# A hybrid decoder layer: constant matmuls ahead of the first product, and another order at its end

## The chip, the core and the metric

The kernel runs on one core of a Trainium2 chip. Its time is device time in microseconds (us) of one execution; the time before is the median of three executions, 1987.16 us (1986.9 to 1989.67). The profile is of one more execution, which took 1982.96 us.

The engines are named as in the profile. PE does matmuls, and PEld loads their stationary operand. DVE works elementwise with up to two tensor operands, ACT elementwise with one operand and a function, POOL here makes a sum over partitions. SP only issues transfers (SPq in the timeline).

## The reference, cut to what matters

```
mod = (silu(c) @ w_ada + b_ada).reshape(B, 6, D)
sh1, sc1, gt1, sh2, sc2, gt2 = mod
h    = rmsnorm(x, g_norm_mix) * (1.0 + sc1) + sh1
proj = h @ w_in
q, k, v, xr, xg = split(proj)          # 1024 columns each
...                                    # attention of q, k, v; recurrence of xr, gated by xg
x = x + gt1 * (mixed @ w_out)
x = x + gt2 * (square(relu(h2 @ w_mlp_in)) @ w_mlp_out)
return rmsnorm(x, g_norm_final)
```

x has 512 tokens of 2048 features, w_in is 2048 x 5120. Only the first two products of w_in are of interest here: the one that makes xr (the first product) and the one that makes the first two heads of q and k and the first four of v (the second).

## The kernel before

Features lie on the 128 partitions and tokens on the free axis, so the 2048 features are 16 **blocks** (k from 0 to 15). Every f32 operand is split into a high half, rounded to the type the matmul takes, and a low half, the difference; ACT makes the high half and DVE the low half. A product of two split operands takes three matmuls: weight high by x high (line L259), weight high by x low (L262), weight low by x high (L263), in the helper `mm3`. A block of a product is 8 outputs of 3 matmuls of 128x512, which is 24, and each output has one of the eight PSUM banks.

**The first product** (the loop over k behind `banks = ...`) multiplies w_in's columns for xr by x times g(1 + sc1), without the norm's factor for each token: that factor (r1) and the shift are put in later, in `conv`. In block k the program names the work for block k+1:

- `weights1(k + 1)`: two transfers of 256 KB on SP (L236), two copies on ACT (L244) and two subtractions on DVE (L122). The transfers are pinned, and the rest has an urgency of up to 150.
- `load_x`: a block of x of 256 KB (L372), its square on ACT (L361) and the running sum `acc` on DVE (L362). In the kernel before it runs two blocks ahead up to k = 4, and three from there.
- `prep1(k + 1)`: a row of sc1, which is a product of a row of w_ada with silu(c) and its sum, done on DVE in two halves of 1024 columns (L211) and put together in L220; then the scale (L380), the high half of x on ACT (L382) and the low half on DVE (L383). The row products load the next rows, 512 KB a half, on SP (L199, pinned).
- at k = 12 the norm starts: POOL sums `acc` over the partitions (L336). At k = 14 ACT and DVE make r1 of it (L345 to L354). Both are marked with an urgency of 250.

**The second product** takes h itself, with norm and shift. `prep2(k)` makes its operand: a row of sh1 (L211, L220), scale and norm on DVE (L389), high half on ACT (L391), low half on DVE (L392). `prep2(0)` and `prep2(1)` are named in block 15 of the first product, and each further one two blocks ahead. Its weights come by `weights` without a pin. Its banks are those of the first product, which ACT empties first (L443).

What sets the order on each engine: the framework walks the whole program in its own estimate of time, and gives an engine the ready instruction that stands earliest in the program. `high_priority(offset=n)` moves an instruction n places forward in that rank, and `later(ins)` pins it behind the instruction that the program names before it on the same engine. Engines work in the order that this makes, also when on the chip the next one is not ready and a later one is. So an instruction on ACT that waits for a transfer holds up all that stands behind it.

At the very start two matmuls with one row of the operand spread c over the partitions (L176), and ACT takes silu of it (L177).

Of the kernel before, what the change touches and what calls it, by code (L numbers as in the profile page):

```python
# [12 lines left out]
AF = mybir.ActivationFunctionType  # L13
ALU = mybir.AluOpType
PSUM = bass.MemoryType.PSUM

P = 128
S = 512
D = 2048
NK = D // P  # L20
HEADS = 8
AW = 1024
# [19 lines left out]
URGENT = 150  # L42
EVAC = 88
PAD, SHIFT = 8, 16

# [17 lines left out]
def hybrid_layer_kernel(  # L65
# [32 lines left out]
    def T(tag, dt=F32, cols=None):  # L98
        return new(next(split_tag) if tag == "w4" else tag, dt, cols)
# [6 lines left out]
    def bank(tag):  # L106
        count[0] += 1
        return pp.tile([P, S], F32, tag=tag, name=f"ps_{tag}_{count[0]}", bufs=PBUFS[tag])

    def const(cols, name, dt=F32):  # L110
        return sp.tile([P, cols], dt, tag=name, name=name)

    act = nc.scalar.activation
    stt = nc.vector.scalar_tensor_tensor
    tt = nc.vector.tensor_tensor
    mm = nc.tensor.matmul

    def f32(ap):
        return ap.bitcast(F32)

    def low(out, full, high):
        tt(out=out, in0=full, in1=f32(high), op=ALU.subtract)  # L122

    def split(full, tag):
        h = T(tag, F32R)
        act(h, full, AF.Copy)
        lo = T(tag, F32R)
        low(lo, full, h)
        return h, lo
# [3 lines left out]
    ones, ntri, nones_r = const(P, "ones"), const(P, "ntri", F32R), const(P, "nones_r", F32R)  # L133
# [14 lines left out]
    def col(base, j):  # L148
        return vec[:, base + j : base + j + 1]
# [15 lines left out]
    nc.vector.memset(ones, 1.0)  # L165
    nc.vector.memset(eps, EPS)


    crow = T("tt")
    nc.sync.dma_start(crow[0:1, :1024], c[:, 1024:])  # L170
# [2 lines left out]
    for i in range(2):  # L173
        v = slice(i * S, (i + 1) * S)
        ps = bank("mm")
        mm(ps, ones[0:1, :], crow[0:1, v], start=True, stop=True)  # L176
        act(cb[1][:, v], ps, AF.Silu)  # L177

    def later(ins):
        return tc.keep_in_program_order(ins)  # L180


    def mod(m, j):
        return mods[:, m * NK + j : m * NK + j + 1]
# [42 lines left out]
    tags2 = [MID]  # L227


    def weights(src, tag=None, urgent=URGENT, pin=False):  # L230

        n = src.shape[-1] if len(src.shape) == 2 else src.shape[1] * src.shape[2]
        with tc.high_priority(offset=urgent):
            r = T("wr" if tag not in ("w3", "w4", "ts") else "raw")
            dst = r[:, :n] if len(src.shape) == 2 else r[:, :n].rearrange("p (a b) -> p a b", b=src.shape[2])
            dma = nc.sync.dma_start(dst, src)  # L236
            if pin:
                later(dma)
            if tag in ("w4", "ts"):
                both = T(tag, F32R)  # L240
                h, lo = both[:, :S], both[:, S : 2 * S]
            else:
                h, lo = T(tag or "wh", F32R), T(tag or "wl", F32R)
            act(h[:, :n], r[:, :n], AF.Copy)  # L244
            low(lo[:, :n], r[:, :n], h[:, :n])
        return h, lo

    class Half:
# [9 lines left out]
    def mm3(out, wh, wl, ah, al, start, stop, pin=False, **kw):  # L258
        first = mm(out, wh, ah, start=start, stop=False, **kw)  # L259
        if pin:  # L260
            later(first)
        mm(out, wh, al, start=False, stop=False, **kw)  # L262
        mm(out, wl, ah, start=False, stop=stop, **kw)  # L263

    def blk(o):
        return slice(o * P, (o + 1) * P)


    class Lane:
# [8 lines left out]
        def next(self):  # L278
            if not self.queue:
                return False  # L280
            try:
                self.wait += next(self.queue[0]) or 0.0
            except StopIteration:
                self.queue.pop(0)
            return True
# [47 lines left out]
    def rnorm_steps(accs, n, ptag, tok=slice(0, S), r=None):  # L333
        m = T("n")[:, tok]
        if ptag is None:
            nc.gpsimd.partition_all_reduce(m, accs[0][:, tok], channels=P, reduce_op=bass_isa.ReduceOp.add)  # L336
            ps = m
        else:
            ps = (bank(ptag) if accs else ptag)[:, tok]
            for i, acc in enumerate(accs or []):  # L340
                mm(ps, ones, acc[:, tok], start=i == 0, stop=i == len(accs) - 1)
        yield
        r_ = T("n") if r is None else r
        r = r_[:, tok]
        ins = act(r, ps, AF.Ln, bias=eps[:, 0:1], scale=1.0 / n)  # L345
        if ptag is None:
            later(ins)
        ins = nc.vector.tensor_scalar(out=m, in0=ps, scalar1=1.0 / n, scalar2=EPS, op0=ALU.mult, op1=ALU.add)
        if ptag is None:
            later(ins)  # L350
        act(r, r, AF.Exp, scale=-0.5)
        tt(out=m, in0=m, in1=r, op=ALU.mult)
        stt(out=m, in0=m, scalar=-0.5, in1=r, op0=ALU.mult, op1=ALU.mult)
        stt(out=r, in0=m, scalar=1.5, in1=r, op0=ALU.add, op1=ALU.mult)  # L354
        yield r_
# [11 lines left out]
    xs, xhl, hT = {}, {}, {}  # L367

    def load_x(k):
        xs[k] = T("a")  # L370
        with tc.high_priority(offset=XPRI):
            ins = nc.sync.dma_start(xs[k], xT[blk(k), :])  # L372
            if k == 0:
                later(ins)
        add_square(acc, xs[k], T("n"), k == 0)

    def prep1(k, tags):
        rows.row(SC1, k, tags)
        g = gm1[:, k : k + 1]
        stt(out=g, in0=mod(SC1, k), scalar=1.0, in1=col(C_GMIX, k), op0=ALU.add, op1=ALU.mult)  # L380
        h, lo = T("a", F32R), T("a", F32R)
        act(h, xs[k], AF.Copy, scale=g)  # L382
        stt(out=lo, in0=xs[k], scalar=g, in1=f32(h), op0=ALU.mult, op1=ALU.subtract)  # L383
        xhl[k] = h, lo

    def prep2(k):
        rows.row(SH1, k, EARLY)
        t = xs[k]
        stt(out=t, in0=t, scalar=gm1[:, k : k + 1], in1=r1, op0=ALU.mult, op1=ALU.mult)  # L389
        h, lo = T("a", F32R), T("a", F32R)  # L390
        act(h, t, AF.Identity, bias=mod(SH1, k))  # L391
        stt(out=lo, in0=t, scalar=mod(SH1, k), in1=f32(h), op0=ALU.add, op1=ALU.subtract)  # L392
        hT[k] = (h, lo)
# [9 lines left out]
    def weights1(k, halves=(0, 1)):  # L403
        return [weights(w_in[blk(k), XR + i * 512 : XR + (i + 1) * 512], tag="a", urgent=min(k * 28, URGENT), pin=True) for i in halves]

    RPRI = 250
    EARLY = itertools.cycle(["x", "tt"] * 3 + ["x"])
    banks = [bank(t) for t in BANKS]
    rows.load(2, EARLY)
    load_x(0)  # L410
    w = weights1(0, [0])
    prep1(0, None)
    w += weights1(0, [1])
    load_x(1)
    rows.load(2, EARLY)
    for k in range(NK):
        if k + 1 < NK:
            w_next = weights1(k + 1)
            for j in (2, 3) if k == 4 else (2,) if k < 4 else (3,):
                if k + j < NK:  # L420
                    load_x(k + j)
            if k + 3 == NK - 1:
                with tc.high_priority(offset=RPRI):
                    r1_gen = rnorm_steps([acc], D, None)
                    next(r1_gen)
            if k + 1 == NK - 1:
                with tc.high_priority(offset=RPRI):
                    r1 = next(r1_gen)
            prep1(k + 1, EARLY)
            if k % 4 == 4 - 1:  # L430
                rows.load(1, EARLY)
        else:
            prep2(0)
            prep2(1)
        for hf in range(2):
            wh, wl = w[hf]
            for o in range(4):
                mm3(banks[hf * 4 + o], wh[:, blk(o)], wl[:, blk(o)], *xhl[k], k == 0, k == NK - 1)
        w = w_next
# [6 lines left out]


    qk, vt, o_t = {}, {}, []
    src_qk = w_in[:, : 2 * AW].rearrange("k (a b) -> k a b", a=2)

    def src_v(k, h0, n):
        return w_in[blk(k), 2 * AW + h0 * P : 2 * AW + (h0 + n) * P]

    def qk_evac(bs, h0, os=range(4)):
        for b in os:
            h, lo = T("a", F32R), T("a", F32R)
# [34 lines left out]
    for k in range(NK):  # L491
        if k + 2 < NK:
            prep2(k + 2)
        wh, wl = weights(src_qk[blk(k), :, : 2 * P])
        for o in range(4):
            mm3(banks[o], wh[:, blk(o)], wl[:, blk(o)], *hT[k], k == 0, k == NK - 1)
        v_mm(banks[4:], weights(src_v(k, 0, 4)), k)
# [322 lines left out]
    def out_evac(outs, g, tok, held=None):  # L820
# [35 lines left out]
        out=gm2, in0=mods[:, SC2 * NK : (SC2 + 1) * NK], scalar=1.0, in1=vec[:, C_GMLP : C_GMLP + NK],  # L856
        op0=ALU.add, op1=ALU.mult,
# [360 lines left out]
    for g in range(1, NG):  # L1218
# [4 lines left out]
        with tc.high_priority(offset=SETE):  # L1223
            r = [T("a") for _ in range(4)]
# [34 lines left out]
    for i, (n, ps) in enumerate(parts):  # L1259
# [15 lines left out]
        src = lambda q: w_blocks[ORDER[q] // 2][ORDER[q] % 2][:, :, n * 512 : (n + 1) * 512]  # L1275
# [195 lines left out]
```

## Time and profile before

| what | us |
|---|---|
| median of three runs | 1987.16 |
| profiled execution, its own time | 1982.96 |
| its span, first to last instruction | 1981.3 |
| PE busy | 1936.3 (98%) |
| DVE busy | 1760.7 (89%) |
| ACT busy | 1077.1 (54%) |

The span and everything in the timeline count from the first instruction. A timeline row gives the start, the time, the engine, the line in the kernel, the operation, its output and inputs, their shapes, how many instructions the row has, and in brackets how long the engine sat idle before it and what ended that. A windows row gives the stretch, and for PE, PEld, DVE, ACT and POOL the busy time with the number of instructions, then the granted clock of PE, the busy share of the 16 DMA engines, and GB/s.

### The profile page before, as it was taken

The numbers are of one execution on the slowest core, as the hardware profiler recorded it, in microseconds if no ns is written. First come the engines' busy times: TensorE is split into PE (matmuls) and PEld (weight loads), VectorE is DVE, ScalarE is ACT, GpSimd is POOL, SyncE is SP. The second block draws the span as 40 slices with busy tenths as digits, with TensorE's granted clock in tenths as the row PEclk, the third lists the DMA queues.
The fourth block names the chain that finished last, engine by engine and source line by source line (L and its number), as shares of the span: only waits on it lengthen the run. The fifth ranks groups of instructions, "written<-read, shape, count | busy, mean of one in ns | idle before, by whom it ended". The sixth has DMA issues, their size and how long they took to land.

```text
span 1981.3 us, 37180 instructions
## 1 busy us (share of the span) xinstructions
PE 1936.3 (98%) x14148; PEld 1813.5 (92%) x14148; DVE 1760.7 (89%) x2979; ACT 1077.1 (54%) x1580; POOL 193.4 (10%) x307
## 2 busy tenths in 40 slices
PE   8999999999999998999999999999999999999997
PEld 6778888788888998999999999999999999999996
DVE  8998786888998599999999999999989779879986
ACT  4443564786433386565555556556445545555542
POOL 0000000000000000112112211200000210211100
PEclk9999999999999999999999999999999999999998
DMA  9896655556779543756656665755677667669653
GB/s 365 306 331 214 205 172 186 183 157 217 226 244 373 176 139 114 239 187 223 211 182 196 223 194 184 235 186 195 234 260 284 247 249 269 232 248 343 215 198 112
DMA packets 205238, 443.51 MB, mean 224 GB/s; under 512 B 20481, under 2 KB 42113, under 8 KB 205058
## 3 DMA queue, kind: packets, MB, share of 16 engines
q1 hardware_dynamic: 176338, 356.58, 54.4%
q0 software_dynamic: 23680, 77.61, 10.6%
q10 hardware_dynamic: 5040, 6.93, 1.1%
q8 instruction: 111, 1.82, 0.4%
q14 instruction: 69, 0.57, 0.1%
HBM read 376.30 MB, written 64.75 MB: 223 GB/s over the span
## 4 chain that ended last, share of the span: by engine, by line
PE 53%; DVE 3%; DMA 1%; issue 1%; ACT 1%; POOL 0%; DVEq 0%; POOLq 0%; ACTq 0%; SPq 0%
PE ps_mm L1104 9%; PE ps_mm L1102 9%; PE ps_mm L1103 9%; PE ps_z L1103 7%; PE ps_z L1104 7%; PE ps_z L1102 7%; PE ps_o L1104 2%; PE ps_o L1102 2%; PE ps_o L1103 2%; DVE w L122 1%; DVE ts L1060 0%; DMA a<-sum 0%; DMA a<-part 0%; DVE a L1357 0%; DVE a L122 0%
## 5 line engine op out<-in xcount | busy, mean ns | idle before, releaser
L1102 PE MATMUL ps_mm<-a,w 128*128 128x256 f32 x1696 | 467.7, 276 | 1.5 <-ACT w L1072 0.5
L1103 PE MATMUL ps_mm<-a,w 128*128 128x256 f32 x1696 | 468.2, 276 | 0.3 <-DVE a L122 0.3
L1104 PE MATMUL ps_mm<-a,w 128*128 128x256 f32 x1696 | 468.1, 277 | 0.3 <-DVE w L122 0.3
L1104 PE MATMUL ps_z<-a,w 128*128 128x256 f32 x1304 | 361.1, 277 | 6.9 <-DVE w L122 6.7
L1103 PE MATMUL ps_z<-a,w 128*128 128x256 f32 x1304 | 360.7, 277 | 0.2
L1102 PE MATMUL ps_z<-a,w 128*128 128x256 f32 x1304 | 360.7, 277 | 0.1
L1072 ACT ACTIVATE w<-ts 128x1024 fp32r<-128x1024 f32 x244 | 258.2, 1058 | 169.6 <-DVE ts L1068 158.0
L1066 ACT ACTIVATE w<-raw 128x768 fp32r<-128x768 f32 x244 | 205.1, 841 | 259.5 <-PE ps_mm L1103 81.7
L122 DVE TENSOR_TENSOR w<-ts,w 128x1024 fp32r<-128x1024 f32 x244 | 297.7, 1220 | 52.9 <-PE ps_mm L1103 16.7
L1102 PEld LDWEIGHTS ps_mm<-a,w 128*128 128x128 f32 x1696 | 318.2, 188 | 2.1 <-ACT w L1072 0.7
L1104 PEld LDWEIGHTS ps_mm<-a,w 128*128 128x128 f32 x1696 | 318.4, 188 | 0.8 <-DVE w L122 0.7
L1103 PEld LDWEIGHTS ps_mm<-a,w 128*128 128x128 f32 x1696 | 318.5, 188 | 0.5 <-DVE a L122 0.5
L122 DVE TENSOR_TENSOR w<-raw,w 128x768 fp32r<-128x768 f32 (+1 forms) x296 | 267.2, 904 | 41.1 <-ACT w L244 24.9
L1104 PEld LDWEIGHTS ps_z<-a,w 128*128 128x128 f32 x1304 | 245.2, 188 | 8.2 <-DVE w L122 8.1
L1103 PEld LDWEIGHTS ps_z<-a,w 128*128 128x128 f32 x1304 | 245.3, 188 | 0.8 <-DVE a L122 0.8
L1102 PEld LDWEIGHTS ps_z<-a,w 128*128 128x128 f32 x1304 | 245.3, 188 | 0.5 <-ACT ps_z L1090 0.3
L244 ACT ACTIVATE wh<-wr 128x512 fp32r<-128x512 f32 (+1 forms) x184 | 113.2, 618 | 144.3 <-PE ps_mm L262 61.8
L259 PE MATMUL ps_mm<-a,wh 128*128 128x512 f32 x448 | 176.1, 393 | 2.4 <-ACT wh L244 1.2
L263 PE MATMUL ps_mm<-a,wl 128*128 128x512 f32 x448 | 174.8, 391 | 0.9 <-DVE wl L122 0.7
L262 PE MATMUL ps_mm<-a,wh 128*128 128x512 f32 x448 | 174.6, 390 | 0.0
L1060 DVE TENSOR_TENSOR ts<-raw 128x512 f32<-128x512 f32 x244 | 166.5, 683 | 6.4 <-DMA raw<-in_w_mlp_out_dram 5.6
L122 DVE TENSOR_TENSOR wl<-wr,wh 128x512 fp32r<-128x512 f32 (+1 forms) x184 | 123.5, 673 | 30.5 <-ACT wh L244 30.2
(334 smaller groups left out, 4011.2 us busy)
## 6 DMA issues: line engine op xcount, KB each, us to landing
raw<-in_w_mlp_out_dram SPq DMA_DIRECT2D x124, 512.0 KB, 4.6
raw<-in_w_mlp_in_dram SPq DMA_DIRECT2D x120, 512.0 KB, 3.8
x<-in_w_adaT_dram SPq DMA_DIRECT2D x108, 512.0 KB, 5.4
wr<-in_w_in_dram SPq DMA_DIRECT2D x160, 256.0 KB, 3.3
tt<-in_w_adaT_dram SPq DMA_DIRECT2D x52, 512.0 KB, 6.4
part<-a POOLq DMA_DIRECT2D x84, 256.0 KB, 4.2
a<-part SPq DMA_DIRECT2D x84, 256.0 KB, 6.2
n<-in_w_adaT_dram SPq DMA_DIRECT2D x64, 256.0 KB, 4.2
```

Source lines behind the costliest of these rows:

```text
L122: tt(out=out, in0=full, in1=f32(high), op=ALU.subtract)
L244: act(h[:, :n], r[:, :n], AF.Copy)
L259: first = mm(out, wh, ah, start=start, stop=False, **kw)
L262: mm(out, wh, al, start=False, stop=False, **kw)
L263: mm(out, wl, ah, start=False, stop=stop, **kw)
L1060: tt(out=t[:, : 2 * HT].rearrange("p (a b) -> p a b", a=2), in0=r[:, HT : 3 * HT].rearrange("p (a b) -> p a b", a=2), in1=r[:, q_(0)].unsq ...
L1066: act(h, r[:, HT:], AF.Copy)
L1072: act(h, t, AF.Copy)
L1102: mm(out, wh[:, blk(i)], ah, start=st, stop=False, **kw)
L1103: mm(out, wh[:, blk(i)], al, start=False, stop=False, **kw)
L1104: mm(out, wl[:, blk(i)], ah, start=False, stop=j == js[-1], **kw)
```

## The change

The two matmuls of c are pinned, and twelve matmuls of the constant `ones` (128 columns, f32, into the bank of tag "o", which nothing reads) are pinned behind them. From k = 8 on, x is loaded four blocks ahead instead of three, so the sum over partitions is named at k = 11 and r1 at k = 13, one block earlier than before. For blocks 13, 14 and 15 the two instructions that split x (L382, L383) get an urgency of 250. `prep2(0)` moves from block 15 to the end of the preparation in block 14, with the same urgency, and the first weight of the second product is loaded right behind it: its transfer, its copy and its subtraction are each pinned behind what the program names before them on SP, ACT and DVE.

```diff
+WARM = 12
...
     def low(out, full, high):
-        tt(out=out, in0=full, in1=f32(high), op=ALU.subtract)
+        return tt(out=out, in0=full, in1=f32(high), op=ALU.subtract)
...
-        mm(ps, ones[0:1, :], crow[0:1, v], start=True, stop=True)
+        later(mm(ps, ones[0:1, :], crow[0:1, v], start=True, stop=True))
         act(cb[1][:, v], ps, AF.Silu)
-
-    def later(ins):
-        return tc.keep_in_program_order(ins)
-
+    warm = bank("o")
+    for _ in range(WARM):
+        later(mm(warm[:, :P], ones, ones, start=True, stop=True))
...
-    def weights(src, tag=None, urgent=URGENT, pin=False):
+    def weights(src, tag=None, urgent=URGENT, pin=False, chain=False):
...
-            if pin:
+            if pin or chain:
                 later(dma)
...
-            act(h[:, :n], r[:, :n], AF.Copy)
-            low(lo[:, :n], r[:, :n], h[:, :n])
+            ins = act(h[:, :n], r[:, :n], AF.Copy), low(lo[:, :n], r[:, :n], h[:, :n])
+            if chain:
+                for i in ins:
+                    later(i)
...
         h, lo = T("a", F32R), T("a", F32R)
-        act(h, xs[k], AF.Copy, scale=g)
-        stt(out=lo, in0=xs[k], scalar=g, in1=f32(h), op0=ALU.mult, op1=ALU.subtract)
+        with tc.high_priority(offset=RPRI if k > NK - 4 else 0):
+            act(h, xs[k], AF.Copy, scale=g)
+            stt(out=lo, in0=xs[k], scalar=g, in1=f32(h), op0=ALU.mult, op1=ALU.subtract)
...
             w_next = weights1(k + 1)
-            for j in (2, 3) if k == 4 else (2,) if k < 4 else (3,):
+            for j in (2,) if k < 4 else (2, 3) if k == 4 else (3,) if k < 8 else (3, 4) if k == 8 else (4,):
                 if k + j < NK:
                     load_x(k + j)
-            if k + 3 == NK - 1:
+            if k + 4 == NK - 1:
                 with tc.high_priority(offset=RPRI):
                     r1_gen = rnorm_steps([acc], D, None)
                     next(r1_gen)
-            if k + 1 == NK - 1:
+            if k + 2 == NK - 1:
                 with tc.high_priority(offset=RPRI):
                     r1 = next(r1_gen)
             prep1(k + 1, EARLY)
+            if k + 1 == NK - 1:
+                with tc.high_priority(offset=RPRI):
+                    prep2(0)
+                w_qk = weights(src_qk[blk(0), :, : 2 * P], chain=True)
             if k % 4 == 4 - 1:
                 rows.load(1, EARLY)
         else:
-            prep2(0)
             prep2(1)
...
-        wh, wl = weights(src_qk[blk(k), :, : 2 * P])
+        wh, wl = weights(src_qk[blk(k), :, : 2 * P]) if k else w_qk
```

More of the change, by code (lines that the diff above doesn't have):

```diff
@@ L166, in hybrid_layer_kernel, with later @@
     nc.vector.memset(eps, EPS)
+    def later(ins):
+        return tc.keep_in_program_order(ins)
     crow = T("tt")
@@ L406, in hybrid_layer_kernel, with src_v @@
     RPRI = 250
+    src_qk = w_in[:, : 2 * AW].rearrange("k (a b) -> k a b", a=2)
+    def src_v(k, h0, n):
+        return w_in[blk(k), 2 * AW + h0 * P : 2 * AW + (h0 + n) * P]
     EARLY = itertools.cycle(["x", "tt"] * 3 + ["x"])
@@ L448, in hybrid_layer_kernel @@
     qk, vt, o_t = {}, {}, []
-    src_qk = w_in[:, : 2 * AW].rearrange("k (a b) -> k a b", a=2)
-    def src_v(k, h0, n):
-        return w_in[blk(k), 2 * AW + h0 * P : 2 * AW + (h0 + n) * P]
     def qk_evac(bs, h0, os=range(4)):
```

## The prediction

> **What bounds the kernel now.** I read the page first, then busy time by windows, then the order of time on each engine around the first product, and last what each engine waited for there.
>
> ```profile
> span 1981.3 us, 37180 instructions
> PE 1936.3 (98%) x14148; PEld 1813.5 (92%) x14148; DVE 1760.7 (89%) x2979; ACT 1077.1 (54%) x1580; POOL 193.4 (10%) x307
> ...
> 11.69:97.90 86.21, 85.48 (x360) 69.34 (x360) 84.17 (x162) 38.94 (x64) 4.57 (x3) 1.00 0.92 344
> 97.90:106.77 8.87, 5.91 (x26) 4.43 (x25) 8.22 (x15) 3.63 (x8) 0.00 (x0) 1.00 0.91 312
> 106.77:193.90 87.13, 87.13 (x384) 72.15 (x385) 79.93 (x142) 34.84 (x58) 0.00 (x0) 1.00 0.79 271
> ```
>
> PE is busy 98% of the span, so only its holes and a slow clock are to be had. The window rows cover the first product up to its last block, the handoff, and the second product. In the second, PE is busy for all of its 87.13 us: 384 matmuls, 0.2269 us each, so a block of 24 takes 5.445 us. In the first, DVE is busy for 84.17 of 86.21 us and the DMA engines 0.92 of the time. Three resources are nearly full at once, and that decides most of what follows.
>
> ```profile
> 2.39 3.75 PE L176 MATMUL ps_mm<-tt,ones 1*128 1x512 f32 x4 [2.39 <-DMA tt<-in_c_dram]
> 11.69 0.80 PE L259 MATMUL ps_mm<-a,a 128*128 128x512 f32 x1 [5.55 <-ACT a L382]
> 12.47 0.79 PE L262 MATMUL ps_mm<-a,a 128*128 128x512 f32 x1
> 13.06 0.63 PE L263 MATMUL ps_mm<-a,a 128*128 128x512 f32 x1
> 13.49 0.63 PE L259 MATMUL ps_mm<-a,a 128*128 128x512 f32 x1
> ...
> 18.35 0.39 PE L259 MATMUL ps_z<-a,a 128*128 128x512 f32 x1
> 18.58 0.40 PE L262 MATMUL ps_z<-a,a 128*128 128x512 f32 x1
> ...
> 20.41 1.07 PE L259 MATMUL ps_mm<-a,a 128*128 128x512 f32 x4
> ```
>
> Block 0 starts at half speed: starts lie 0.43 us apart at 13.06 and 0.23 apart from 18.35 on. (The column of the granted clock reads 1.00 here, so the slow start must be read from the spacing.) PE idles 5.55 us ahead of it. Block 1 starts at 20.41.
>
> ```profile
> 63.93 0.39 PE L259 MATMUL ps_mm<-a,a 128*128 128x512 f32 x1
> 64.44 0.50 PE L262 MATMUL ps_mm<-a,a 128*128 128x512 f32 x1
> 69.78 0.62 PE L259 MATMUL ps_mm<-a,a 128*128 128x512 f32 x2
> ...
> 63.64 0.75 DVE L383 SCALAR_TENSOR_TENSOR a<-a,gm,a 128x512 fp32r<-128x512 f32 x1
> ```
>
> In block 9 the second matmul waits: it needs the low half of x's operand, which DVE finishes at 64.39, and PE goes on at 64.44. From there PE's time is DVE's, whatever came before.
>
> ```profile
> 86.72 4.11 POOL L336 PARTITION_ALL_REDUCE n<-n  x1 [76.00 <-DVE n L362]
> 84.03 1.29 DVE L122 TENSOR_TENSOR a<-wr,a 128x512 fp32r<-128x512 f32 x2
> 87.76 2.07 DVE L220 SCALAR_TENSOR_TENSOR mods<-ga,vec 128x1 f32<-128x1 f32 x1
> 89.87 0.16 DVE L380 SCALAR_TENSOR_TENSOR gm<-mods,vec 128x1 f32<-128x1 f32 x1
> 91.09 1.41 DVE L122 TENSOR_TENSOR a<-wr,a 128x512 fp32r<-128x512 f32 x2
> 92.43 0.74 DVE L383 SCALAR_TENSOR_TENSOR a<-a,gm,a 128x512 fp32r<-128x512 f32 x1
> 94.23 1.21 DVE L211 SCALAR_TENSOR_TENSOR x<-x,cb 128x1024 f32<-128x1024 f32 x1
> 95.51 1.28 DVE L122 TENSOR_TENSOR a<-wr,a 128x512 fp32r<-128x512 f32 x2
> 96.72 0.41 DVE L348 TENSOR_SCALAR n<-n 128x512 f32<-128x512 f32 x1
> 98.86 0.68 DVE L353 SCALAR_TENSOR_TENSOR n<-n,n 128x512 f32<-128x512 f32 x1
> ...
> 85.76 0.71 ACT L382 ACTIVATE a<-a,gm 128x512 fp32r<-128x512 f32 x1
> 99.53 0.63 ACT L244 ACTIVATE wh<-wr 128x512 fp32r<-128x512 f32 x1 [3.05 <-DMA wr<-in_w_in_dram]
> 100.07 0.71 ACT L382 ACTIVATE a<-a,gm 128x512 fp32r<-128x512 f32 x1
> ...
> 93.22 0.50 PE L262 MATMUL ps_mm<-a,a 128*128 128x512 f32 x1 [0.61 <-DVE a L383]
> 100.82 1.19 PE L259 MATMUL ps_mm<-a,a 128*128 128x512 f32 x4 [2.75 <-ACT a L382]
> 106.77 0.50 PE L259 MATMUL ps_mm<-a,wh 128*128 128x512 f32 x1 [0.21 <-ACT a L443]
> ```
>
> The tail of the product: block 14 waits 0.61 us for L383 of DVE, although its input from ACT (85.76) had been there since 86.5; DVE did other things first. Block 15 waits 2.75 us for L382 of ACT at 100.07, whose scale (L380) had been there since 90.0; it stood behind a weight copy of the next product (99.53) that waited for its transfer. The second product then waits 0.21 us.
>
> **The change, part by part.** The sum is made against the profiled execution, 1982.96 us with a span of 1981.3. The median of the runs is 1987.16, 4.2 us more; I take the difference off that median.
>
> *Twelve constant matmuls.* They add f32 matmuls of 128 columns behind c's two. The nearest rows:
>
> ```profile
> 241.97 1.84 PE L542 MATMUL ps_z<-ones,x 128*128 128x2 f32 x16
> ```
>
> Eight such matmuls of two columns made 16 records, two each, 0.115 us a record at full clock. So twelve make 24 records, 2.8 us at full clock and, if it doubles, 5.5 at half. They follow c's at 6.14 and end by about 11.6, inside the hole that ends at 11.69: nothing on the path. The other end is the half-speed spacing of 0.43 for each of the 24 records, 10.3 us, to 16.4. Block 0 at full clock then ends at 21.9, 1.4 us later than now, and 1.1 of it is left where block 9 waits today (0.51 between its first two starts, at 63.93 and 64.44, where 0.23 is usual).
>
> What they may bring: PE busy from c's matmuls on, so the clock is up by 11.69. The first three matmuls still wait for operands up to 13.06; 22 more starts at 0.227 put block 1 at 18.06 instead of 20.41, a lead of 2.35 us. I count it as **0**: block 9's second matmul still waits for L383 at 64.39, and the change gives no priority to L383 before block 13. The lead becomes 2.35 us of longer waits up to block 9. If this cover is gone, because DVE comes to L383 earlier, the lead is kept: between 0 and -2.35.
>
> [...]
>
> *x a block further from block 8.* It moves one x transfer of 256 KB (on SP, ahead of that block's rows), one square on ACT and one add on DVE ahead of block 9's and 10's operands. With DMA at 344 GB/s in the window row, 256 KB is 0.76 us, and it falls away again once all x are in. Block 10 starts at 69.78 with little to spare behind DVE, so the price is between 0 and 0.8; I take **+0.2**, near the low end, since only the first block behind it pays and the x of a block is not what DVE waits for there.
>
> The all-reduce comes a block earlier with it. Its cost stays: at 87.76 a DVE instruction of one column takes 2.07 us, inside POOL's 86.72 to 90.83. It now falls before block 13's weight splits (84.03), not behind them. That is part of the new wait below.
>
> *The last operands and the next product's first.* Without waits, block 10 at 69.78 plus six blocks of 5.445 us puts the second product at 102.45. It starts at 106.77, so 4.3 us are lost: 0.61, 2.75 and 0.21 in the idle column, and the rest in slow restarts (a matmul behind a wait takes 0.50). L382 and L383 of blocks 13 to 15 now come first, and the copies of the next product's first weight stand behind prep2(0) on ACT and DVE. That removes the cause of all three: **-4.3**.
>
> Moved with it: prep2(0) issues two row products, their sum, two operand instructions on DVE, one on ACT and two row loads of 512 KB on SP; w_qk issues one transfer on SP, pinned behind those loads, one ACT copy and one DVE subtraction, pinned too. Behind the pinned ACT copy stand the evacuations of the eight banks; behind the pinned transfer stand the v weights of block 0.
>
> What is late next is **the weights' low halves**. They are ranked behind what is now urgent. Block 15's are made from 95.51, the first ready at 96.2. PE without waits wants them with the third matmul of block 15, at 69.78 + 5 x 5.445 + 0.45 = 97.45. Put ahead of them L383 of block 15 and the four steps of the norm (0.41 at 96.72 and three like the one at 98.86): back to back, instructions of 0.68 start 0.60 apart, as the two in the 1.28 us at 95.51 show, so this is 0.66 + 0.33 + 1.8 = 2.8 us. They come at 99.0, a wait of **1.5** us, which I take, since it needs no other move. Bounds: if the second product's row products, of 1.15 us the half (94.23, until the splits at 95.51 with the sum between), go behind them, 2.3 us are won back and the wait is 0.5 at most, or none with one more; if instead prep2(0)'s two operands and the low half of w_qk go ahead too, 1.9 more, the wait is 3.4. So 0 to 3.4.
>
> The second product's own supply has room:
>
> ```profile
> 111.97 0.74 DVE L392 SCALAR_TENSOR_TENSOR a<-a,mods,a 128x512 fp32r<-128x512 f32 x1
> ...
> 117.80 0.39 PE L259 MATMUL ps_mm<-a,wh 128*128 128x512 f32 x1
> ```
>
> Block 2's operand is done at 112.7 and used at 117.8, so PE may come about 3 to 4 us earlier without waiting. The stages behind are PE's own chain, and the gain goes on to the end.
>
> Sum: 0 + 0.2 - 4.3 + 1.5 = **-2.6 us**: 1980.3 in the profile's terms, **1984.5** against the median.
>
> **The rivals.**
>
> *The lead of the clock is kept and the tail is clean.* DVE's order comes from the scheduler's own estimate of readiness; earlier x and earlier matmuls may bring L383 of block 9 forward. For it: DVE idles only 2 of 86 us, yet it makes operands just before use and runs rows ahead, so there is order to be gained. Against it: nothing in blocks 0 to 8 is re-ranked. -4.3 - 2.35 = -6.65, **1980.5**.
>
> *DVE takes it all.* Low halves of blocks 13, 14 and 15 all wait behind the all-reduce, the norm and prep2(0): waits up to 3.4 us, 0.8 for the x, and part of the old handoff. About 0: **1987.2**. This is also the case in which the change doesn't do what it says.
>
> *Slower: a new hole at the start of the MLP.* The whole program's order is made in one pass, so a shifted front may reorder later stages.
>
> ```profile
> 760.00:780.00 20.00, 14.21 (x117) 13.70 (x116) 19.76 (x41) 12.42 (x19) 0.00 (x0) 0.98 0.31 95
> 780.00:800.00 20.00, 19.93 (x158) 19.63 (x158) 17.49 (x27) 10.25 (x15) 4.08 (x6) 0.94 0.56 186
> ...
> 779.02 0.46 PE L1104 MATMUL ps_z<-a,w 128*128 128x256 f32 x1 [4.11 <-DVE w L122]
> ```
>
> There PE is busy 14.21 of 20 us, DVE 19.76, and one wait is 4.11 us; the granted clock of 0.98 and 0.94 in the two rows is 0.4 + 1.2 = 1.6 us of full speed lost behind it. Against a second such hole: this one has its place, and DVE had slack just before. One more costs 4.1 + 1.6 = 5.7; less the tail's 2.6 that is +3.1, **1990.3**, and 1993 if the tail's gain is gone too. It decides from the point where DVE's next weight split there is over 2.6 us later than now.
>
> **How the numbers follow.** Forecast 0.45, its own range -4.3 to -1, 1982.9 to 1986.2; kept lead 0.27; DVE takes all 0.15; new hole 0.13. What can be told from no change is 0.2%, 4.0 us. Faster by more: the kept lead, 0.27, and the forecast's near edge with a clean tail, 0.14, so 0.41. Slower by more: most of the new hole, 0.09. The rest, 0.50, is within. The range from 1979.0 to 1990.0 reaches to the kept lead and to most of the hole, and leaves out about 0.1 on each side.
>
> **What would show it.** Right: starts 0.23 apart from the beginning of block 0; block 9's second matmul still at 64.4, with longer waits before it; L382 of block 15 near 91 instead of 100; the second product's first matmul at 103 to 105 with PE's waits in blocks 13 to 15 ended by L122 of DVE. Wrong: block 10 well before 69.8 (the lead is kept), a half-speed block 0 (the constants don't do their part), a first matmul held beyond 12 us by the constants, or an end whose distance from the second product's start differs by more than 2 us from now (later stages were reordered).

## The result, and the profile after

| | before, us | changed, us |
|---|---|---|
| median of 22 runs each | 1984.35 (1981.03 to 1989.67) | 1982.27 (1978.15 to 1987.21) |
| ratio of the two, 95% interval | | 0.9986 (0.9980 to 0.9992) |
| profiled execution, its own time | 1982.96 | 1981.67 |
| its span | 1981.3 | 1979.9 |
| second product's first matmul | 106.77 | 105.86 |
| from there to the end of the span | 1874.5 | 1874.1 |

The ratio is -2.8 us (-4.0 to -1.6); -2.6 had been forecast. That is less than the 0.2% (4.0 us) that were set as the bound of what can be told from no change, so by that bound the time is the same. The two profiled executions lie 1.3 us apart, and the front of the program, up to the second product, gives 0.9 of it. The time came out where it was forecast; the way to it did not, as the rows show. (Two executions ran far slower than all others and are left out of the ratios: one of the kernel before, 6493.36 us, and the profiled one of the run "once more" of the order with the banks emptied first, 2408.51 us at a granted clock of 0.752.)

The span, the busy times and the windows that answer to those of before (columns: stretch, its length, busy time and instructions of PE, PEld, DVE, ACT, POOL, then granted clock, DMA share, GB/s), from the profile after:

```profile
span 1979.9 us, 37227 instructions
PE 1939.2 (98%) x14172; PEld 1817.4 (92%) x14172; DVE 1760.6 (89%) x2979; ACT 1076.6 (54%) x1580; POOL 193.3 (10%) x307
...
11.30:100.43 89.13, 84.84 (x361) 68.52 (x362) 87.41 (x166) 39.83 (x67) 4.56 (x3) 0.98 0.96 355
...
105.86:192.68 86.82, 86.82 (x385) 71.91 (x383) 79.08 (x140) 33.62 (x56) 0.00 (x0) 1.00 0.79 271
```

The picture of before is kept: PE full in the second product, DVE (87.41 of 89.13 us) and DMA (0.96) full in the first. New is the granted clock of 0.98 in the first row; it was 1.00. 0.02 of 89.13 us is 1.8 us of full speed lost somewhere in the first product.

The timeline after, at the start and around blocks 9 and 10. (The lines of the first product stand one to six further down: the weight by x high is now L264, by x low L267, and L383 is now L389.)

```profile
6.32 4.69 PE L184 MATMUL ps_o<-ones 128*128 128x128 f32 x24
11.30 1.20 PE L264 MATMUL ps_mm<-a,a 128*128 128x512 f32 x4 [0.28 <-ACT a L388]
12.33 0.39 PE L267 MATMUL ps_mm<-a,a 128*128 128x512 f32 x1
...
17.26 0.50 PE L264 MATMUL ps_mm<-a,a 128*128 128x512 f32 x1 [0.21 <-ACT a L388]
18.05 0.49 PE L267 MATMUL ps_mm<-a,a 128*128 128x512 f32 x1 [0.29 <-DVE a L389]
...
63.60 0.50 PE L267 MATMUL ps_mm<-a,a 128*128 128x512 f32 x1 [1.03 <-DVE a L389]
68.95 1.07 PE L264 MATMUL ps_mm<-a,a 128*128 128x512 f32 x4
...
62.80 0.74 DVE L389 SCALAR_TENSOR_TENSOR a<-a,gm,a 128x512 fp32r<-128x512 f32 x1
```

The constants are 24 records in 4.69 us and end inside the hole. Block 0 runs at 0.23 between starts, and block 1 begins at 17.26 instead of 20.41. Of these 3.15 us, 0.39 are the start of block 0. The lead shrinks wherever an operand is late: by 0.7 at block 1 (the waits of 0.21 and 0.29, and slow matmuls behind them), by 0.7 at block 5 (block 6 begins at 45.87 instead of 47.61), and by 0.9 at block 9, whose second matmul waits for DVE's low half, now 1.03 us. Block 10 begins at 68.95, 0.83 earlier than before. That says little by itself: a second profile of the kernel before, further down, has block 10 at 68.82.

The tail after, from the timeline, and one row of the windows:

```profile
80.33 4.11 POOL L341 PARTITION_ALL_REDUCE n<-n  x1 [69.67 <-ACT a L247]
...
80.11 1.22 DVE L214 SCALAR_TENSOR_TENSOR x<-x,cb 128x1024 f32<-128x1024 f32 x1
81.25 3.25 DVE L214 SCALAR_TENSOR_TENSOR tt<-tt,cb 128x1024 f32<-128x1024 f32 x1
84.90 1.21 DVE L214 SCALAR_TENSOR_TENSOR x<-x,cb 128x1024 f32<-128x1024 f32 x1
86.05 1.28 DVE L123 TENSOR_TENSOR a<-wr,a 128x512 fp32r<-128x512 f32 x2
87.25 0.73 DVE L389 SCALAR_TENSOR_TENSOR a<-a,gm,a 128x512 fp32r<-128x512 f32 x1
...
80.19 0.71 ACT L388 ACTIVATE a<-a,gm 128x512 fp32r<-128x512 f32 x1
90.75 0.71 ACT L388 ACTIVATE a<-a,gm 128x512 fp32r<-128x512 f32 x1
...
88.04 0.50 PE L267 MATMUL ps_mm<-a,a 128*128 128x512 f32 x1 [2.38 <-DVE a L389]
88.68 0.63 PE L264 MATMUL ps_mm<-a,a 128*128 128x512 f32 x1
105.86 0.39 PE L264 MATMUL ps_mm<-a,wh 128*128 128x512 f32 x1
```

```profile
88.50:92.00 3.50, 3.50 (x10) 2.70 (x9) 3.46 (x9) 1.87 (x3) 0.00 (x0) 0.51 0.93 261
```

The old waits of 0.61, 2.75 and 0.21 at blocks 14, 15 and the handoff are gone, and one of 2.38 has come at block 13. The high half of its x was there at 80.9; its low half was made at 87.25, because DVE first did a row product that took 3.25 instead of 1.22 us while POOL summed over partitions, another row product of 1.21, and the block's two weight splits. Behind the wait the clock fell to half for 3.4 us: 10 matmuls lie between 88.5 and 92.0, where 3.50 us by 0.227 makes 15. Blocks 14 and 15 run without a wait. Six blocks of 5.445 from 68.95 end at 101.62, so the tail still loses 4.24 us; before it lost 4.32.

### The profile page after: what moved, and what is told of

Its sections match the earlier page's. It is cut to its first block, busy times and chain, and to the rows that moved or that the text cites. A ratio compares the mean times of both kernels' runs of the same rounds, so it can differ in the third digit from the quotient of the medians.

```text
span 1979.9 us, 37227 instructions
## 1 busy us (share of the span) xinstructions
PE 1939.2 (98%) x14172; PEld 1817.4 (92%) x14172; DVE 1760.6 (89%) x2979; ACT 1076.6 (54%) x1580; POOL 193.3 (10%) x307
## 4 chain that ended last, share of the span: by engine, by line
PE 52%; DVE 4%; DMA 1%; issue 1%; ACT 1%; POOL 0%; DVEq 0%; SPq 0%; POOLq 0%; ACTq 0%
PE ps_mm L1113 9%; PE ps_mm L1111 9%; PE ps_mm L1112 9%; PE ps_z L1112 7%; PE ps_z L1113 6%; PE ps_z L1111 6%; PE ps_o L1113 2%; PE ps_o L1112 2%; PE ps_o L1111 2%; DVE w L123 1%; DMA raw<-in_w_mlp_out_dram 1%; DVE a L1366 1%; DVE ts L1069 0%; DVE a L123 0%; DVE a L1301 0%
## 5 line engine op out<-in xcount | busy, mean ns | idle before, releaser
L123 DVE TENSOR_TENSOR w<-ts,w 128x1024 fp32r<-128x1024 f32 x244 | 298.2, 1222 | 52.6 <-PE ps_mm L1112 14.1
L123 DVE TENSOR_TENSOR w<-raw,w 128x768 fp32r<-128x768 f32 (+1 forms) x296 | 267.9, 906 | 40.2 <-ACT w L247 22.3
L264 PE MATMUL ps_mm<-a,wh 128*128 128x512 f32 x448 | 175.9, 393 | 3.0 <-DVE a L469 2.4
L267 PE MATMUL ps_mm<-a,wh 128*128 128x512 f32 x448 | 174.8, 390 | 0.0
L214 DVE SCALAR_TENSOR_TENSOR x<-x,cb 128x1024 f32<-128x1024 f32 x108 | 131.4, 1221 | 22.9 <-DMA x<-in_w_adaT_dram 22.8
```

The costliest lines, as they stand in the source:

```text
L123: return tt(out=out, in0=full, in1=f32(high), op=ALU.subtract)
L214: ins = stt(out=t, in0=t, scalar=1.0, in1=cb[q_], op0=ALU.mult, op1=ALU.mult, accum_out=self.ga[:, q_ : q_ + 1],)
```

## The experiments

All ratios below are against runs of the kernel before on the same chip. Line numbers shift from kernel to kernel, so the text names the instruction where it matters. The theory that the profile after suggests: the constants' lead is lost at block 9 whatever follows, because DVE is full and comes to the low half last; and the tail's gain is eaten at block 13, by DVE's order and by the all-reduce that fell into it. The rivals: the constants alone bring the gain; or the order of the tail alone brings it.

### The constants alone

```diff
 kernel before, and
+    warm = bank("o")
+    for _ in range(WARM):
+        later(mm(warm[:, :P], ones, ones, start=True, stop=True))
```

> The kernel before with the twelve constant matmuls alone. Theory (from block 9 on PE's time is DVE's): block 0 starts 0.23 us apart, the lead of some 2.3 us turns into waits up to block 9, block 10 starts at 69.0 to 69.8, the second product at 106 to 106.8 as before, and the time is that of the kernel before within 1 us. Rival (PE keeps the lead): block 10 near 67.4, the second product near 104.4, 2.3 us faster.

Ratio 0.9986 (0.9977 to 0.9995). Its waits from 60 to 110 us (engine, output and line that waited, what ended it; us in all, times, longest), and from the timeline the second product's start:

```profile
PE ps_mm L265 <- DVE a L386: 1.7, 2, 1.0
```

```profile
99.98 1.69 PE L262 MATMUL ps_mm<-a,a 128*128 128x512 f32 x4 [2.17 <-ACT a L385]
107.15 0.39 PE L262 MATMUL ps_mm<-a,wh 128*128 128x512 f32 x1
```

The lead is lost by block 9 here too (1.04 us of wait for L386 of DVE, the low half of x), and block 10 begins at 69.50. Block 15 waits for ACT again, 2.17 us, now with a half-speed stretch behind it (starts 0.43 us apart at 103.17 and 103.60), so the second product begins at 107.15, not earlier than before. Yet the time is 2.8 us shorter, where the theory had at most 1 us.

It was run a second time:

> The constants alone once more, beside it. By the front's trace (second product at 107.15 with a clock drop, 105.4 without) it should be at 0.999 to 0.9998; if the constants are the gain of the whole change, it stays at 0.9985 or below.

0.9988 (0.9979 to 0.9996); block 10 at 68.82, the wait at block 15 3.20, the second product at 107.46. The same twice: a shorter time, and no gain at the second product. The ratio lies between the two values that were set, 0.999 and 0.9985, so this run does not choose between them.

### The change without the constants

```diff
 changed kernel, without
-    warm = bank("o")
-    for _ in range(WARM):
-        later(mm(warm[:, :P], ones, ones, start=True, stop=True))
```

> The changed kernel without the constant matmuls. Theory: block 0 at half speed, hardly a wait at block 9, block 10 within 0.9 us of the changed kernel's 68.95, the second product within 1 us of its 105.86 (a clock drop behind block 13's wait left aside, which costs 1.7 us where it falls). Rival (the constants are the gain): 2.3 us later from block 10 on and about 2.3 us slower, at the time of the kernel before.

1.0003 (0.9995 to 1.0012). From its timeline:

```profile
64.05 0.50 PE L264 MATMUL ps_mm<-a,a 128*128 128x512 f32 x1
106.32 0.39 PE L261 MATMUL ps_mm<-a,wh 128*128 128x512 f32 x1
```

Without them the wait at block 9 is 0.07 instead of 1.03: the lead of the constants is what stood in that wait. Block 10 begins at 69.39. Block 13 has its 2.40, and the half-speed stretch (1.7 us of full speed). The front is the theory's (the second product within 1 us of 105.86), the time is the rival's, that of the kernel before. A second time:

> The changed kernel without the constants once more, since its time (1.0003 of the kernel before) and its trace (the second product at 106.3 with a clock drop of 1.7 us before it) disagree. If the trace of the front is the whole of it, the ratio comes near 0.9985 to 0.9992 this time. If the constants do something that the front's trace doesn't show, it stays at 1.000 or above.

0.9998 (0.9987 to 1.0009), block 10 at 68.88, the second product at 105.70. Again the ratio falls between the two values set, nearer to the second.

### Both kernels once more

The kernel before against itself, and the changed one again, unaltered:

> The kernel before against itself. [...]

> The changed kernel once more, beside it. If its gain of 0.14% is real it stays between 0.998 and 0.9995; its front should again have the 2.4 us wait at block 13, and the second product near 105.9 with a drop of the clock, or 104.2 without.

Before against itself: 1.0004 (0.9993 to 1.0014). Changed: 0.9993 (0.9985 to 1.0002), which is -1.4 us (-3.0 to +0.4). From the timeline of before, the second time:

```profile
99.20 2.08 PE L259 MATMUL ps_mm<-a,a 128*128 128x512 f32 x4 [2.11 <-ACT a L382]
106.38 0.39 PE L259 MATMUL ps_mm<-a,wh 128*128 128x512 f32 x1
```

This time a half-speed stretch does follow the wait of 2.11 us (four matmuls in 2.08 us, where 1.07 is usual); behind the 2.75 us of the first profile there was none. Yet the second product begins 0.39 earlier than there, at 106.38. And of the changed kernel, the second time, the timeline and the stretch that ran at half speed the first time:

```profile
88.24 0.50 PE L267 MATMUL ps_mm<-a,a 128*128 128x512 f32 x1 [2.39 <-DVE a L389]
96.12 0.50 PE L267 MATMUL ps_mm<-a,a 128*128 128x512 f32 x1 [0.54 <-DVE a L389]
105.32 0.39 PE L264 MATMUL ps_mm<-a,wh 128*128 128x512 f32 x1
```

```profile
88.50:92.00 3.50, 3.50 (x16) 2.85 (x16) 3.46 (x9) 1.92 (x3) 0.00 (x0) 1.00 0.85 284
```

The same wait at the same place, 2.39 us, and the clock stays at 1.00: 16 matmuls instead of 10. So the drop does not come with the kernel, nor with the length of the wait alone. It is not worth the 1.7 us of full speed either that the expectation gave it (104.2 without a drop): the second time block 14 caught up with DVE (0.54 at 96.12), and the second product comes only 0.54 earlier.

### The sum over partitions left out

```diff
 changed kernel, in the norm's first call (n == D):
-            nc.gpsimd.partition_all_reduce(m, accs[0][:, tok], ...)
-            ps = m
+            ps = accs[0][:, tok]
```

Every partition then uses its own sum of squares, so r1 and all behind it have other values than the reference; the remaining work is the same.

> The changed kernel with the sum over partitions left out of the first norm: r1 is made from each partition's own sum, so the output is not the reference's. Theory (the all-reduce holds DVE for 2.0 us just ahead of block 13's operands): the 3.25 us of the row product at 81.25 fall to 1.22, L389 of block 13 ends near 86.0 instead of 87.99, its wait falls from 2.38 to about 0.4 us, and no clock drop follows; the second product starts at 102 to 104. Rival (block 13 waits for DVE's order alone, and the held time is made up elsewhere): the second product stays within 0.7 us of 105.86, or of 104.2 without a clock drop.

0.9982 (0.9973 to 0.9990). From the timeline:

```profile
80.99 1.31 DVE L214 SCALAR_TENSOR_TENSOR tt<-tt,cb 128x1024 f32<-128x1024 f32 x1
85.02 0.75 DVE L392 SCALAR_TENSOR_TENSOR a<-a,gm,a 128x512 fp32r<-128x512 f32 x1
...
85.83 0.50 PE L267 MATMUL ps_mm<-a,a 128*128 128x512 f32 x1 [0.44 <-DVE a L392]
93.83 0.50 PE L267 MATMUL ps_mm<-a,a 128*128 128x512 f32 x1 [0.66 <-DVE a L392]
103.05 0.39 PE L264 MATMUL ps_mm<-a,wh 128*128 128x512 f32 x1
```

The row product takes 1.31 instead of 3.25, the wait of block 13 for its low half (L392 here) goes from 2.38 to 0.44, no half-speed stretch follows (starts 0.23 apart from 86.16 on), and the second product begins at 103.05, 2.3 to 2.8 us before the two profiles of the changed kernel. So the all-reduce holds DVE for 2 us, and in this order on DVE that makes 1.9 of the 2.4 us of wait.

### x as far ahead as before

```diff
 changed kernel, with
-            for j in (2,) if k < 4 else (2, 3) if k == 4 else (3,) if k < 8 else (3, 4) if k == 8 else (4,):
+            for j in (2, 3) if k == 4 else (2,) if k < 4 else (3,):
-            if k + 4 == NK - 1:      # the sum over partitions
+            if k + 3 == NK - 1:
-            if k + 2 == NK - 1:      # r1
+            if k + 1 == NK - 1:
```

> The changed kernel with x and the norm where the kernel before has them; the constants, the urgency and the moved prep2(0) and w_qk stay. Theory (the sum over partitions follows the last x and holds DVE for 2 us wherever it falls): block 13 waits at most 0.5 us, since the hold now falls behind its operands; block 14 or 15 waits for DVE instead, 1 to 3 us, and the second product starts at 104 to 106 without a drop of the clock: x a block further ahead moves the wait and gains nothing of its own. Rival (x ahead is what the tail needs): the second product after 106.5.

0.9995 (0.9987 to 1.0004). From the timeline:

```profile
84.09 0.74 DVE L389 SCALAR_TENSOR_TENSOR a<-a,gm,a 128x512 fp32r<-128x512 f32 x1
86.61 2.07 DVE L223 SCALAR_TENSOR_TENSOR mods<-ga,vec 128x1 f32<-128x1 f32 x1
...
92.07 0.50 PE L267 MATMUL ps_mm<-a,a 128*128 128x512 f32 x1 [0.61 <-DVE a L389]
99.72 0.50 PE L267 MATMUL ps_mm<-a,a 128*128 128x512 f32 x1 [0.99 <-DVE a L389]
106.33 0.79 PE L264 MATMUL ps_mm<-a,wh 128*128 128x512 f32 x1 [2.69 <-ACT a L457]
```

Now block 13's low half is made at 84.09, ahead of the instruction that the all-reduce holds (86.61, 2.07 us where 0.22 is usual), and block 13 doesn't wait. Blocks 14 and 15 wait 0.61 and 0.99 for their low halves instead, and the second product waits 2.69 for a bank that ACT had not emptied, since r1 and with it `prep2(0)`, which stands ahead of the banks on ACT, came later; a drop of the clock follows (the matmul at 106.93 takes 0.63 us, where 0.39 is usual), which the theory had ruled out. So x a block further ahead, with the norm that follows it, is what moves the wait to block 13, and it pays for itself behind: with it the second product begins at 105.86 or 105.32, without it at 106.33. (The run takes back x and the norm together; which of the two does it is not separated.) The start lies between the theory's 104 to 106 and the rival's 106.5, and the times don't tell the two kernels apart.

### DVE's row products queued behind the operands

A row of block k+1 may now start only behind the low half of block k, `prep2(0)` and `prep2(1)` only behind that of block 15; the norm's steps are named where they were before the change.

```diff
 changed kernel, with
-            stt(out=lo, in0=xs[k], scalar=g, in1=f32(h), ...)
+            low_x[k] = stt(out=lo, in0=xs[k], scalar=g, in1=f32(h), ...)
...
-            prep1(k + 1, EARLY)
+            with tc.issue_after(low_x[k].ins):
+                prep1(k + 1, EARLY)
...
-                with tc.high_priority(offset=RPRI):
+                with tc.high_priority(offset=RPRI), tc.issue_after(low_x[k + 1].ins):
                     prep2(0)
```

> The changed kernel with another order on DVE: the row products of block k+1 stand behind the low half of x of block k, those of the second product behind block 15's, and the two steps of the norm are named where the kernel before names them. Theory (what is late is DVE's order, not DVE's work): no wait at blocks 5 and 9, the lead of the clock is kept, a wait of at most 0.5 us at block 13, the second product at 100 to 101.5, and 3 to 6 us faster than the changed kernel. Rival (DVE's work or the transfers are the bound): waits of the same sum stand elsewhere, the second product starts after 104, and the time is the changed kernel's.

0.9994 (0.9983 to 1.0004). From the timeline:

```profile
83.97 0.50 PE L267 MATMUL ps_mm<-a,a 128*128 128x512 f32 x1 [0.51 <-DVE a L389]
...
104.17 0.72 ACT L397 ACTIVATE a<-a,mods 128x512 fp32r<-128x512 f32 x1 [3.27 <-DVE mods L223]
104.80 2.04 ACT L459 ACTIVATE a<-ps_mm 128x512 f32<-128x512 f32 x4
...
105.43 0.63 PE L264 MATMUL ps_mm<-a,wh 128*128 128x512 f32 x1 [5.03 <-ACT a L459]
```

In the product itself it does what was meant: no wait at block 9, block 10 at 66.74, 0.51 us at block 13 and none behind it, the last block from 94.80. Then PE stands 5.03 us, because ACT has the high half of `prep2(1)` (L397) ahead of the copies that empty the banks (L459), and its row sum comes late from DVE. All that was won is lost at the handoff, to another engine's queue: the second product begins after 104 and the time is the changed kernel's, as the rival had it.

### And the banks emptied first

```diff
 the kernel above, with prep2(0) and prep2(1) taken out of the loop, and where the banks are emptied:
-        act(t, banks[o], AF.Copy)
+        ins = act(t, banks[o], AF.Copy)
         xr_t.append(t)
+        if o in (3, 7):
+            with tc.issue_after(low_x[NK - 1].ins), tc.issue_after(ins.ins):
+                prep2(o // 4)
+        if o == 3:
+            w_qk = weights(src_qk[blk(0), :, : 2 * P], chain=True)
```

> The order of the run before, and ACT empties the first four banks ahead of prep2(0)'s high half and the other four ahead of prep2(1)'s. In the run before, PE left block 15 at 100.2 and then waited 5.03 us for a bank, because ACT stood at prep2(1), which waited for DVE. Theory (that bank is all that was left): the first product as there, a wait of at most 0.5 us at the handoff, the second product at 100.3 to 101.5, and 6 to 8 us faster than the kernel before. Rival (DVE's and ACT's work for the handoff doesn't fit): the second product after 103 and no more than 3 us faster than the kernel before.

0.9970 (0.9958 to 0.9981). From the timeline:

```profile
80.60 3.25 POOL L341 PARTITION_ALL_REDUCE n<-n  x1 [70.12 <-DVE mods L223]
80.62 2.23 DVE L385 SCALAR_TENSOR_TENSOR gm<-mods,vec 128x1 f32<-128x1 f32 x1
...
83.98 0.74 DVE L389 SCALAR_TENSOR_TENSOR a<-a,gm,a 128x512 fp32r<-128x512 f32 x1
...
96.48 2.64 ACT L452 ACTIVATE a<-ps_mm 128x512 f32<-128x512 f32 x4 [2.55 <-PE ps_mm L268]
99.36 0.73 ACT L397 ACTIVATE a<-a,mods 128x512 fp32r<-128x512 f32 x1 [0.24 <-DVE a L395]
...
84.78 0.50 PE L267 MATMUL ps_mm<-a,a 128*128 128x512 f32 x1 [0.51 <-DVE a L389]
101.04 0.84 PE L264 MATMUL ps_mm<-a,wh 128*128 128x512 f32 x3
```

ACT empties four banks at 96.48, before `prep2(0)` at 99.36, and the second product begins at 101.04 without a wait. The all-reduce holds DVE as long as ever (2.23 us for a column), but with the operand next in the queue that costs PE 0.51 us. The time is 5.9 us shorter than before (3.8 to 8.3), and once more:

> The mended order with the constants once more, since its first time rests on five executions: near 0.997 if that holds, 0.9985 or above if it was chance. Second product at 101 again.

0.9957 (0.9944 to 0.9970), 8.5 us (6.0 to 11.1), from four executions. Its profile does not show where the second product begins at full clock, so the start at 101 rests on one trace. By the time, twice, this order beats the kernel before; against the changed kernel's 0.9986 and 0.9993 it is ahead too.

### That order without the constants

The three lines of the constants are taken out, as above.

> The same without the constant matmuls. Theory (with DVE's order mended PE keeps the lead, so now the constants count): block 0 at half speed, no wait up to block 12, block 10 at 69 to 69.5, the second product 1.5 to 2.5 us later than with them, and as much slower. Rival (the lead is lost in any order): within 0.7 us of the run with them.

0.9976 (0.9968 to 0.9985). From the timeline:

```profile
12.00 0.80 PE L261 MATMUL ps_mm<-a,a 128*128 128x512 f32 x1 [5.63 <-ACT a L385]
15.45 0.39 PE L264 MATMUL ps_mm<-a,a 128*128 128x512 f32 x1
...
101.14 0.84 PE L261 MATMUL ps_mm<-a,wh 128*128 128x512 f32 x3
```

Block 0 starts at half speed (starts 0.43 apart from 13.38 to 14.66), block 10 is 0.74 later than with the constants (68.28 against 67.54), and the second product begins at 101.14 against 101.04. With the wait at block 9 gone the lead lives on to block 13, and ends there: the low half of that block is ready at 84.81 without and at 84.72 with the constants. So for the front the rival was right (within 0.7 us), not the theory (1.5 to 2.5 later). The ratio of 0.9976 lies above both of the order with the constants, but the intervals overlap, so what the constants are worth in the time stays open here too.

### What the runs say together

| kernel | block 10 starts | second product starts | lost between, beyond six blocks of 5.445 | ratio to before |
|---|---|---|---|---|
| before | 69.78, 68.82 | 106.77, 106.38 | 4.3, 4.9 | 1.0004 |
| constants alone | 69.50, 68.82 | 107.15, 107.46 | 5.0, 6.0 | 0.9986, 0.9988 |
| changed, no constants | 69.39, 68.88 | 106.32, 105.70 | 4.3, 4.2 | 1.0003, 0.9998 |
| changed | 68.95, 69.14 | 105.86, 105.32 | 4.2, 3.5 | 0.9986, 0.9993 |
| changed, x as before | 68.64 | 106.33 | 5.0 | 0.9995 |
| changed, no all-reduce | 68.68 | 103.05 | 1.7 | 0.9982 |
| operands first | 66.74 | 105.43 | 6.0 | 0.9994 |
| operands and banks first | 67.54 | 101.04 | 0.8 | 0.9970, 0.9957 |
| the same, no constants | 68.28 | 101.14 | 0.2 | 0.9976 |

Where two values stand in a field, they are of two runs, and "before" in the last column is the kernel against itself. In the first four rows the second product's start and the ratio don't go together. In the traces, by the means of two, the constants alone begin the second product 0.7 us later than before, the change without them 0.6 earlier and the whole change 1.0 earlier. In the times the constants alone have the whole of the gain, twice, and the change without them none, twice. Taking the constants out or in moves no instruction on any engine but PE, and on PE only in blocks 0 and 1. Between the kernel before and the changed one DVE, ACT and SP have some instructions of the second product in another order; from about 190 us on all four have the same order on every engine. Yet the profiled executions take from 1870.6 us (constants alone, the second time) to 1879.4 (no constants, the first time, with three more waits of PE near 255 us) from the second product to the end. Two profiles of each can't average that out, and no run here profiles many executions. **So what part of the 2.8 us comes from the constants, and where, stays open.** What the traces do show is the front, up to the second product.

## Why the prediction was right or wrong

**The time** was right: -2.6 forecast, -2.8 (-4.0 to -1.6) measured, within the bound for no change that had the largest chance. As far as these runs show, that the number itself agrees is luck. All of the -2.6 was to come from the tail and to stand in the second product's start, at 103 to 105; that came at 105.86 and 105.32, by the means of two 1.0 earlier than before. And the constants, which were counted as 0, are the part without which the time is that of the kernel before (1.0003 and 0.9998).

**The constants at 0.** Right for the first product: they end at 11.01 inside the hole (11.6 was estimated), block 0 runs at 0.23, and the lead becomes a longer wait at block 9, 1.03 against 0.07 and 0.34 without them. The second matmul of block 9 was expected at 64.4 still; it is at 63.60, since DVE itself is 0.84 earlier: its low half is done at 63.55, not 64.39. That is not the change: in the second profile of the kernel before it is done at 63.41. Block 1 began at 17.26, not 18.06: block 0 began 0.39 earlier, and PE takes its matmuls in another order, four of L264 first (the row at 11.30), and so doesn't wait for low halves. Whether 0 is right for the whole program is what stays open above. The price of the constants was sized well: 24 records in 4.69 us, between the 2.8 at full clock and the 5.5 at half, with the clock rising within them, at 10.02.

**x a block further at +0.2: mis-sized.** The price was looked for in the transfer, the square and the add. Block 10 is indeed not late. The cost is the all-reduce that comes with it: taken back, block 13's wait of 2.4 us is gone. The prediction had seen that the hold now falls ahead of block 13's weight splits, but counted it into a wait two blocks later. Nor did it count what comes back: with r1 earlier the second product begins 0.5 to 1.0 earlier than without (105.86 and 105.32 against 106.33), so in these traces the part is no cost.

**The tail at -4.3 with a new wait of +1.5.** The three old waits did go, and L388 of ACT for block 15 stands at 90.75, as foreseen. The failed step is "L382 and L383 of blocks 13 to 15 now come first". On DVE they do not: the low half of block 13 stands behind two row products and the weight splits. Built with the urgency on these instructions taken out, the program has every instruction of all five engines in the same place, so the earlier L388 on ACT is not the urgency's doing either but that of the parts that were moved. The likely reason that the urgency does nothing, argued and not shown, is that the scheduler's own estimate of time has them not yet ready at that point, and an urgency only chooses among the ready. So the new wait is not block 15's third matmul behind L122 (now L123), but block 13's second behind L389; and it measured 2.38 us, inside the bounds of 0 to 3.4, and up to 1.7 more where the clock fell behind it, which no term had. Before the change the tail lost 4.3 and 4.9, after it 4.2 and 3.5: the gain is about 0.7, not 2.8.

**The rivals.** The kept lead fell, as did the clean tail. "DVE takes it all" is, in mechanism, the nearest to what the front shows: the wait moved from one late operand to another. Its time, no change, is 2.8 us from the measured one. The new hole at the start of the MLP didn't come: from the second product to the end there are 1874.1 us against 1874.5, within the 2 us that were set as the sign, and from about 190 us on nothing was reordered.

**The second product's room.** Right: it was to bear a start 3 to 4 us earlier, and in the order with the banks emptied first it bears one 5.7 us earlier.

## What to carry to other kernels

Where an engine is full and in order, ask for each operand on the critical path what stands in front of it in that engine's queue: here 2.4 us of waiting were an order, not a lack of time. An urgency may change nothing; a filler named to start only behind the critical instruction does. And after one queue is mended, look at the head of the next one before timing: the 5 us won on DVE were lost to one instruction on ACT until that was moved too.

## What was not expected of the hardware

**A wait of 2.4 us was followed by half speed once, and once not.** After 2.38 us the records show half speed from 88.52 to 91.94, 3.41 us, which cost up to 1.7; after 2.39 us at the same place in another execution the granted clock is 1.00 from 88.5 to 92. Nor was the wait of 2.75 us in the tail of before followed by a drop: there the clock's records have none between 18.01 and 779.18. So not the length of the wait alone decides. In the profiles of the two kernels the times between two changes of the clock, from its first rise on, are whole multiples of 3.413 us: 78.51 from the rise at 10.02 to the drop at 88.52 is 23 of them, 686.08 from 91.94 to 778.01 is 201, and 761.17 in the profile of before, from 18.01 to 779.18, is 223. The drops at 88.52, 778.01 and 779.18 last one each. The rest is an estimate from these records: if such steps go on between the changes, the wait that ended at 88.04 lay within one (85.11 to 88.52), and the one of 2.75 was divided by the end of one at 99.93, into 1.86 and 0.89. That this made the difference is not shown. A start at half speed lasted 6.3 us in the profile of before, 11.69 to 18.01, but 3.4 in the order without the constants, 12.00 to 15.4.

**POOL's sum over partitions holds DVE for 2 us.** The 2.07 at one column was known from the profile of before; new is that a row product is held as long. It took 3.25 us instead of 1.22, and one-column instructions took 2.07 and 2.23 instead of 0.16 to 0.22, each while POOL's instruction ran. With it left out, the row product took 1.31. The traces show a hold of 2 us only, not of the 4.11 that POOL's record spans. Nor does it begin with that record: a row product of DVE that was under way when POOL began at 80.33 took its usual 1.22, and where none was under way, at 80.60, POOL's record is 3.25.
